# Weight sums by DMA issued in a pinned order, with 2048 bytes of scratch for dynamic DMAs

## The chip, the core and the metric

The kernel runs on one core of a Trainium2 chip, in one launch. TensorE (PE) multiplies, VectorE (DVE) and ScalarE (ACT) work elementwise, GpSimd (POOL) does small things and issues some DMAs, SyncE (SP) issues the others; all transfers of the core run on the same 16 DMA engines. The metric is the device time of one execution in microseconds, as the median of several runs. Times below that look like clock readings ("at 242.62") are microseconds from the start of the profiled span.

## What is computed

Two layers of a decoder trunk on 512 tokens of width 1024. Each layer is a feed-forward block, a mixer (attention and retention) and a second feed-forward block, each followed by a layer norm. All arithmetic is float32. The change is in the feed-forward block, which runs four times:

```python
def swiglu_ffn(x, w_gu, w_down):
    a, u = jnp.split(x @ w_gu, 2, axis=-1)
    return (jax.nn.silu(a) * u) @ w_down
...
for l in range(DEPTH):
    x = layer_norm(DEEPNORM_ALPHA * x + 0.5 * swiglu_ffn(x, ffn1_w_gu[l], ffn1_w_down[l]),
                   ln1_g[l], ln1_b[l])
    x = layer_norm(DEEPNORM_ALPHA * x + hybrid_mixer(...), ln2_g[l], ln2_b[l])
    x = layer_norm(DEEPNORM_ALPHA * x + 0.5 * swiglu_ffn(x, ffn2_w_gu[l], ffn2_w_down[l]),
                   ln3_g[l], ln3_b[l])
```

The hidden width (`D_FF`) is 2816, so `w_down` is 2816 x 1024.

## The kernel before

**Precision.** Every operand is split in a rounded high part and a rest: ACT casts the high part (L159, tiles `uh` for weights, `hh` for activations), DVE subtracts it from the source (L160, `ul` and `hl`). A product is then three matmuls on PE (L168 to L170: high by high, high by low, low by high). ACT and DVE each take their instructions in the order in which they stand in the program.

**Weights.** They come by DMA from SP into two buffers `raw`, are split into one of six pairs of buffers (`uh`, `ul`), and are used once. The class `Weights` holds a list of items, one for each pair, and runs up to six items ahead of the matmuls. Which instruction stands where on an engine is then settled by a scheduler when the program is built, except for those that are pinned by `keep_in_program_order`.

**The down projection.** A part of `x @ w_down` is done by a scheme with seven instead of eight block products (Strassen's). It is made of seven steps, each with two halves, one for each of two groups of rows, g = 0 and 1; a half is 12 matmuls. Some steps use a sum of blocks of `w_down` instead of a block. These sums are made by the DMA engines: the two buffers `R[0]` and `R[1]` (one for each group, which reuse the two `S` buffers of the stage ahead) have two halves x = 0 and 1 of 512 KB. SP loads a block into each (L356), and POOL then issues DMAs that add another block onto what is there (`add`, L349, `accum_op=ALU.add`). For each group there are three additions onto half 0, one after the other, and one onto half 1:

- half 0: first sum (used by step 3), second sum (step 4), third sum (step 7). Each addition after the first has to wait until the split of the sum before it (`cut`, ACT L159 `uh<-R`, then DVE L160 `ul<-R`) has read the buffer.
- half 1: its one sum is used by step 6.

So there are eight additions in a feed-forward block, 32 in all, and eight splits of `R`. The texts below number them as they stand on POOL: before the change, additions 1 to 8 are g0 first, g0 half 1, g1 first, g1 half 1, g0 second, g1 second, g0 third, g1 third. Splits 1 to 8 are, on ACT and DVE: first sums of g0 and g1, second sums, halves 1, third sums. The left operand of step 3 is made by `fifth` (L640 to L649), once for each group: DVE subtracts (L645), ACT casts (`hh<-s`), DVE subtracts the rest (`hl<-s`). On ACT the cast for group 1 stands behind split 4.

**POOL** does nothing else around this place. Its other work is a power for each layer norm (L458) and things of the mixer. A DMA that POOL issues is described by POOL in memory set aside for it, `dynamic_dma_scratch_size` bytes in each partition (L1113). The small statistics of norms, attention and retention lie in the pool `small` (L105), with four buffers for each name.

Of the kernel before, what the change touches and what calls it, by code (L numbers as in the profile page):

```python
# [10 lines left out]
ALU = mybir.AluOpType  # L11
# [28 lines left out]
class Weights:  # L40


    def __init__(self, T, items):
        self.T, self.items = T, items
        self.emitted = self.taken = self.out = 0
        self.ready = []
        self.raws = {}
        self.last = {raw: i for i, (raw, _, _, _) in enumerate(items)}
# [44 lines left out]
class Trunk:  # L93
    def __init__(self, tc, ctx):
        self.tc, self.nc = tc, tc.nc
        self.n = 0
        self.now = 0
        self.pin = True
        self.tasks = []
        self.later = []  # L100
        nc = self.nc
        self.base = ctx.enter_context(tc.tile_pool(name="base", bufs=1))
        self.rawp = ctx.enter_context(tc.tile_pool(name="rawp", bufs=2))
        self.unit = ctx.enter_context(tc.tile_pool(name="unit", bufs=UBUFS))
        self.small = ctx.enter_context(tc.tile_pool(name="small", bufs=4))  # L105
        self.psum = ctx.enter_context(tc.tile_pool(name="psum", bufs=8, space=PSUM))
        self.ident = self.base.tile([P, P], F32, name="ident")
        make_identity(nc, self.ident)
        self.mhalf = self.base.tile([P, 8], F32, name="mhalf")
        nc.vector.memset(self.mhalf, -0.5)  # L110
        self.xh = self.base.tile([P, KC, SEQ], F32R, name="xh")
        self.xl = self.base.tile([P, KC, SEQ], F32R, name="xl")
        self.Y = self.base.tile([P, NT, D], F32, name="Y")
# [226 lines left out]
    def down_items(self, w, key, R, row):  # L340

        def block(i, j, g):
            r0 = i * 512 + g * 256
            return w[r0 : r0 + 256, j * 512 : (j + 1) * 512].rearrange("(k p) c -> p k c", p=P)

        def add(g, x, i, j):
            self.nc.gpsimd.dma_start(R[g][:, x], block(i, j, g), accum_op=ALU.add)  # L349

        def begin(go):
            def f(v, hi, lo):
                for g in range(2):
                    R[g] = self.spool.tile([P, 2, 2, 512], F32, tag="S", name=self.nm("R"), bufs=2)
                    for x in range(2):
                        self.nc.sync.dma_start(R[g][:, x], block(0, x, g))  # L356
                    add(g, 0, 0, 1)
                return go(v, hi, lo)
            return f

        def cut(g, x, *after):
            def go(v, hi, lo):
                hv, lv = (t.rearrange("p (k c) -> p k c", k=2) for t in (hi, lo))
                self.split(hv, lv, R[g][:, x])
                for a in after:
                    add(g, *a)
                return hv, lv
            return (None, None, None, go)

        p1, p2, p3 = (self.wide_item(w, j * 512, i, (key, "b", i, j)) for i, j in ((0, 0), (1, 0), (1, 1)))  # L370
        p1[0] = p1[0][:3] + (begin(p1[0][3]),)
        return (p1 + p2 + [cut(g, 0, (0, 1, 1), (1, 1, 1)) for g in range(2)]
                + [cut(g, 0, (0, 1, 0)) for g in range(2)] + p3 + [cut(g, 1) for g in range(2)]
                + [row] + [cut(g, 0) for g in range(2)])

# [751 lines left out]
```

## Time and profile before

| | |
|---|---|
| time, median of 3 runs | 1902.52 us (1901.39 to 1902.53) |
| the profiled execution, its own time | 1903.95 us |
| its span in the trace | 1902.2 us |
| mean granted TensorE clock | 0.981 |
| busy: PE, DVE, ACT, POOL | 96%, 71%, 46%, 7% |
| additions by DMA (L349) in a row, each feed-forward block | 8, the first at 226.1, 806.3, 1169.3 and 1747.7 |

The span runs from the first to the last instruction in the trace; the execution's own time is 1.75 us longer. PE is busy nearly all the time, so that what matters is the few places where it waits, and the clock that it is granted there. A row of the timeline gives the start, the duration, the engine, the line, the operation, output and input, how many instructions are merged, and in brackets how long the engine had been idle and what ended that. A row of the chain of work that ended last gives a start, a duration and what was done; "issue" is time in which the engine waited for nothing that the profile shows. A row of the waits gives the microseconds in total, the number of times and the longest.

### The profile page before, as it was taken

The numbers are of one execution on the slowest core, as the hardware profiler recorded it, in microseconds if no ns is written. First come the engines' busy times: TensorE is split into PE (matmuls) and PEld (weight loads), VectorE is DVE, ScalarE is ACT, GpSimd is POOL, SyncE is SP. The second block draws the span as 40 slices with busy tenths as digits, with TensorE's granted clock in tenths as the row PEclk, the third lists the DMA queues.
The fourth block names the chain that finished last, engine by engine and source line by source line (L and its number), as shares of the span: only waits on it lengthen the run. The fifth ranks groups of instructions, "written<-read, shape, count | busy, mean of one in ns | idle before, by whom it ended". The sixth has DMA issues, their size and how long they took to land.

```text
span 1902.2 us, 29290 instructions
## 1 busy us (share of the span) xinstructions
PE 1823.9 (96%) x12074; PEld 1657.7 (87%) x12074; DVE 1341.5 (71%) x1942; ACT 879.6 (46%) x1439; POOL 124.3 (7%) x104
## 2 busy tenths in 40 slices
PE   9999969999999999969999999699999999999698
PEld 9999958897789999958899999588877899999586
DVE  7788756655758788756688887646567687887655
ACT  4455534168623455534235554432785234555330
POOL 0000010110110000010000000101111100000101
PEclk9999989999999999989999999899999999999899
DMA  5242564232222223365322236541232122425631
GB/s 177 89 134 90 160 130 168 74 95 79 55 89 81 97 89 126 120 148 173 99 66 91 90 105 190 127 155 62 78 90 89 45 89 91 132 89 166 140 116 45
DMA packets 151989, 205.87 MB, mean 108 GB/s; under 512 B 4656, under 2 KB 116016, under 8 KB 151856
## 3 DMA queue, kind: packets, MB, share of 16 engines
q1 hardware_dynamic: 143152, 187.23, 30.4%
q0 software_dynamic: 8704, 16.78, 5.5%
q8 instruction: 94, 1.54, 0.3%
q14 instruction: 39, 0.32, 0.1%
HBM read 201.89 MB, written 2.10 MB: 107 GB/s over the span
## 4 chain that ended last, share of the span: by engine, by line
PE 77%; issue 10%; DVE 5%; DMA 3%; ACT 2%; POOL 2%; SPq 0%; POOLq 0%; DVEq 0%; ACTq 0%
PE ps L170 25%; PE ps L169 25%; PE ps L168 25%; DMA R<-in_ffn_w_down_dram 1%; ACT sw L896 1%; POOL sw L898 1%; DMA raw<-in_ffn_w_gu_dram 1%; POOL R L349 1%; PE ps L426 1%; DVE Y L462 1%; DVE st L452 1%; DVE ul L160 1%; ACT uh L159 1%; DVE Y L459 1%; DVE Y L450 0%
## 5 line engine op out<-in xcount | busy, mean ns | idle before, releaser
L168 PE MATMUL ps<-xh,uh 128*128 128x256 f32 (+1 forms) x1616 | 482.7, 299 | 0.7 <-ACT uh L159 0.7
L169 PE MATMUL ps<-xl,uh 128*128 128x256 f32 (+1 forms) x1616 | 480.0, 297 | 0.6 <-DVE xl L160 0.6
L170 PE MATMUL ps<-xh,ul 128*128 128x256 f32 (+1 forms) x1616 | 479.7, 297 | 0.4 <-DVE ul L160 0.4
L159 ACT CAST uh<-raw 128x1024 fp32r<-128x1024 f32 (+1 forms) x325 | 291.1, 912 | 229.7 <-PE ps L169 149.3
L160 DVE TENSOR_TENSOR ul<-raw,uh 128x1024 fp32r<-128x1024 f32 (+1 forms) x325 | 336.7, 1049 | 83.5 <-ACT uh L159 83.0
L170 PE MATMUL ps<-Th,ul 128*128 128x256 f32 x1152 | 326.0, 283 | 0.0
L168 PE MATMUL ps<-Th,uh 128*128 128x256 f32 x1152 | 326.0, 283 | 0.0
L169 PE MATMUL ps<-Tl,uh 128*128 128x256 f32 x1152 | 326.0, 283 | 0.0
L168 PEld LDWEIGHTS ps<-xh,uh 128*128 128x128 f32 x1616 | 309.3, 191 | 11.1 <-issue 1.6
L170 PEld LDWEIGHTS ps<-xh,ul 128*128 128x128 f32 x1616 | 309.1, 191 | 9.2 <-DVE ul L160 0.8
L169 PEld LDWEIGHTS ps<-xl,uh 128*128 128x128 f32 x1616 | 309.3, 191 | 8.7 <-DVE xl L160 1.2
L168 PE MATMUL ps<-uh,hh 128*128 128x512 f32 x640 | 254.5, 398 | 56.4 <-ACT hh L159 56.4
L170 PE MATMUL ps<-uh,hl 128*128 128x512 f32 x640 | 254.1, 397 | 5.5 <-DVE hl L160 5.5
L169 PE MATMUL ps<-ul,hh 128*128 128x512 f32 x640 | 253.1, 395 | 0.0
L160 DVE TENSOR_TENSOR ul<-S,uh 128x1024 fp32r<-128x1024 f32 x144 | 175.8, 1221 | 72.8 <-ACT uh L159 72.4
L159 ACT CAST uh<-S 128x1024 fp32r<-128x1024 f32 x144 | 151.0, 1048 | 160.5 <-PE ps L169 159.2
L168 PEld LDWEIGHTS ps<-Th,uh 128*128 128x128 f32 x1152 | 221.2, 192 | 0.0
L169 PEld LDWEIGHTS ps<-Tl,uh 128*128 128x128 f32 x1152 | 221.2, 192 | 0.0
L170 PEld LDWEIGHTS ps<-Th,ul 128*128 128x128 f32 x1152 | 221.2, 192 | 0.0
L168 PEld LDWEIGHTS ps<-uh,hh 128*128 128x128 f32 x640 | 122.9, 192 | 83.3 <-ACT hh L159 58.1
L170 PEld LDWEIGHTS ps<-uh,hl 128*128 128x128 f32 x640 | 122.4, 191 | 35.4 <-DVE hl L160 10.1
L169 PEld LDWEIGHTS ps<-ul,hh 128*128 128x128 f32 x640 | 122.7, 192 | 25.6
(141 smaller groups left out, 2248.5 us busy)
## 6 DMA issues: line engine op xcount, KB each, us to landing
raw<-in_ffn_w_gu_dram SPq DMA_DIRECT2D x86, 1024.0 KB, 5.5
raw<-in_ffn_w_down_dram SPq DMA_DIRECT2D x40, 1024.0 KB, 5.1
raw<-in_w_in_dram SPq DMA_DIRECT2D x18, 1024.0 KB, 5.4
R<-in_ffn_w_down_dram POOLq DMA_DIRECT2D x32, 512.0 KB, 6.0
R<-in_ffn_w_down_dram SPq DMA_DIRECT2D x16, 512.0 KB, 5.9
raw<-in_w_in_dram SPq DMA_DIRECT2D x8, 512.0 KB, 5.1
raw<-in_w_out_dram SPq DMA_DIRECT2D x8, 512.0 KB, 6.1
raw<-in_w_out_dram SPq DMA_DIRECT2D x4, 1024.0 KB, 5.0
```

The lines of the kernel that those rows point to most:

```text
L159: a = self.nc.scalar.copy(hi, src)
L160: b = self.nc.vector.tensor_sub(lo, src, hi.bitcast(F32))
L168: mm(out, ah, bh, start=start, stop=False, **kw)
L169: mm(out, ah, bl, start=False, stop=False, **kw)
L170: mm(out, al, bh, start=False, stop=stop, **kw)
L349: self.nc.gpsimd.dma_start(R[g][:, x], block(i, j, g), accum_op=ALU.add)
L426: nc.tensor.transpose(b[:, c * P : (c + 1) * P], src[:, c * P : (c + 1) * P], self.ident)
L452: nc.vector.bn_stats(out=st[:, h, :], in_=y[:, hs])
L459: nc.vector.scalar_tensor_tensor(out=y, in0=y, scalar=mv[:, 0:1], in1=g, op0=ALU.subtract, op1=ALU.mult)
L462: nc.vector.scalar_tensor_tensor(out=y[:, hs], in0=y[:, hs], scalar=rs, in1=b[:, hs], op0=ALU.mult, op1=ALU.add)
L896: nc.scalar.copy(sw[q * 32 : q * 32 + 32, :n], src[o * 32 : o * 32 + 32, :n])
L898: nc.gpsimd.tensor_mul(sw[:, :n], sw[:, :n], S)
```

## The change

- Each addition is pinned behind what stands before it on POOL's queue (`keep_in_program_order`).
- The additions onto half 1 are written with the first ones, ahead of all splits, and no longer behind split 1 and split 2.
- The scratch for dynamic DMAs grows from 1024 to 2048 bytes in each partition, and the pool `small` has three buffers for each name, no longer four.

```diff
-        self.small = ctx.enter_context(tc.tile_pool(name="small", bufs=4))
+        self.small = ctx.enter_context(tc.tile_pool(name="small", bufs=3))
...
         def add(g, x, i, j):
-            self.nc.gpsimd.dma_start(R[g][:, x], block(i, j, g), accum_op=ALU.add)
+            self.tc.keep_in_program_order(self.nc.gpsimd.dma_start(R[g][:, x], block(i, j, g), accum_op=ALU.add))
...
                     add(g, 0, 0, 1)
+                for g in range(2):
+                    add(g, 1, 1, 1)
                 return go(v, hi, lo)
...
-        return (p1 + p2 + [cut(g, 0, (0, 1, 1), (1, 1, 1)) for g in range(2)]
+        return (p1 + p2 + [cut(g, 0, (0, 1, 1)) for g in range(2)]
                 + [cut(g, 0, (0, 1, 0)) for g in range(2)] + p3 + [cut(g, 1) for g in range(2)]
...
-    nc = _bacc.Bacc("TRN2", target_bir_lowering=False, num_devices=1, dynamic_dma_scratch_size=1024)
+    nc = _bacc.Bacc("TRN2", target_bir_lowering=False, num_devices=1, dynamic_dma_scratch_size=2048)
```

On POOL, in the first feed-forward block, these rows stood before the change (`R_2638` is the buffer of group 0, `R_2642` that of group 1; a row with x2 is two additions in a row, onto half 0 and onto half 1):

```order
L349 DMA R_2638<-in_ffn_w_down_dram 128x2x512 x2
L349 DMA R_2642<-in_ffn_w_down_dram 128x2x512 x2
L349 DMA R_2638<-in_ffn_w_down_dram 128x2x512
L349 DMA R_2642<-in_ffn_w_down_dram 128x2x512
L349 DMA R_2638<-in_ffn_w_down_dram 128x2x512
L349 DMA R_2642<-in_ffn_w_down_dram 128x2x512
L458 TENSOR_TENSOR rs_3494<-ve_3492,mhalf 128x1
```

The scheduler had thus already put the additions onto half 1 ahead of the second sums. With the change the same place on POOL reads:

```order
L349 DMA R_2638<-in_ffn_w_down_dram 128x2x512
L349 DMA R_2642<-in_ffn_w_down_dram 128x2x512
L349 DMA R_2638<-in_ffn_w_down_dram 128x2x512
L349 DMA R_2642<-in_ffn_w_down_dram 128x2x512
L349 DMA R_2638<-in_ffn_w_down_dram 128x2x512
L349 DMA R_2642<-in_ffn_w_down_dram 128x2x512
L349 DMA R_2638<-in_ffn_w_down_dram 128x2x512
L349 DMA R_2642<-in_ffn_w_down_dram 128x2x512
L460 TENSOR_TENSOR rs_3494<-ve_3492,mhalf 128x1
```

One pair has changed places: the first sum of group 1 is now the second addition, and half 1 of group 0 the third. The additions 4 to 8 stand where they stood. The other three blocks read in the same way.

On ACT, at the splits of `R` in the first block, these rows stood before (`uh<-R` are splits 1 to 4, `hh<-s_328` the casts of `fifth`):

```order
L159 CAST uh_2770<-R_2638 128x1024
L159 CAST hh_2792<-hT_145 128x512
L159 CAST hh_2796<-hT_145 128x512
L159 CAST hh_2818<-s_328_2791 128x512
L159 CAST uh_2812<-R_2642 128x1024
L159 CAST uh_2837<-R_2638 128x1024
L159 CAST uh_2842<-R_2642 128x1024
L159 CAST hh_2849<-s_328_2791 128x512
L159 CAST uh_2868<-raw_2679 128x1024
```

And with the change:

```order
L159 CAST uh_2772<-R_2638 128x1024
L159 CAST hh_2793<-hT_145 128x512
L159 CAST hh_2797<-hT_145 128x512
L159 CAST hh_2818<-s_328_2792 128x512
L159 CAST uh_2813<-R_2642 128x1024
L159 CAST uh_2837<-R_2638 128x1024
L159 CAST uh_2842<-R_2642 128x1024
L159 CAST hh_2849<-s_328_2792 128x512
L159 CAST uh_2868<-raw_2681 128x1024
```

Nothing has moved here but numbers in names, nor has anything on DVE, PE or SP in the whole program: POOL's pair is the only difference in order.

## The prediction

> **What bounds the kernel now.** PE is busy 96% of the span, so I began with what PE waits for. The view of waits, for PE, is headed by these rows:
>
> ```profile
> PE ps L168 <- ACT hh L159: 56.4, 4, 14.3
> PE ps L170 <- DVE hl L160: 5.5, 8, 1.3
> ```
>
> Four waits of about 14.1 us, one in each feed-forward block, are nearly all that PE waits. Next I read the chain of work that ended last, at the first of them (start, duration, what):
>
> ```profile
> 240.79 1.22 DVE ul L160
> 242.01 0.61 DVE hl L160
> 242.62 1.21 POOL R L349
> 243.83 5.13 issue
> 248.98 1.23 POOL R L349
> 250.21 4.99 issue
> 255.22 1.21 POOL R L349
> 256.43 5.05 issue
> 261.50 5.95 DMA R<-in_ffn_w_down_dram
> 267.53 1.05 ACT uh L159
> 268.60 1.23 DVE ul L160
> ...
> 270.43 0.61 DVE hl L160
> 271.09 0.79 PE ps L170
> ```
>
> The chain is four additions by DMA in single file (additions 3, 4, 5 and 6), then split 4, then PE. Why PE waits for an `hh` cast is seen on ACT (its timeline):
>
> ```profile
> 248.74 1.05 ACT L159 CAST uh<-R 128x1024 fp32r<-128x1024 f32 x1 [6.59 <-DMA R<-in_ffn_w_down_dram]
> ...
> 268.48 0.61 ACT L159 CAST hh<-s 128x512 fp32r<-128x512 f32 x1
> ```
>
> The cast of group 1 for step 3 stands behind splits 3 and 4 and cannot start until addition 6 has landed, though step 3 itself needs only first sums. So the time at which addition 6 lands sets the end of the wait.
>
> What holds the additions apart? Two pairs of starts on POOL's timeline, in the first and in the second block, and how long the earlier of each pair took from issue to landing (the DMA view of windows 232:233 and 813:814):
>
> ```profile
> 226.13 1.35 POOL L349 DMA_DIRECT2D R<-in_ffn_w_down_dram  x1 [224.82 <-DVE Q L530]
> 232.47 1.23 POOL L349 DMA_DIRECT2D R<-in_ffn_w_down_dram  x1 [4.99 <-issue]
> ...
> 813.64 1.23 POOL L349 DMA_DIRECT2D R<-in_ffn_w_down_dram  x1 [6.14 <-DMA R<-in_ffn_w_down_dram]
> 821.84 1.21 POOL L349 DMA_DIRECT2D R<-in_ffn_w_down_dram  x1 [6.98 <-issue]
> ```
>
> ```profile
> R<-in_ffn_w_down_dram POOLq DMA_DIRECT2D x1, 512.0 KB, 9.9
> ```
>
> ```profile
> R<-in_ffn_w_down_dram POOLq DMA_DIRECT2D x1, 512.0 KB, 7.9
> ```
>
> 232.47 + 9.9 = 242.4, and addition 3 starts at 242.62; 813.64 + 7.9 = 821.5, and the next starts at 821.84. Each addition starts 0.2 to 0.3 us after the one before it has landed, whether that took 6 or 10 us, and also where its own data had long been there (addition 4 needs only a plain load). I read this as room for one addition in the scratch: the next can be described only when the last is done.
>
> **The change part by part.** The scratch doubles. If one addition fits in 1024 bytes and two don't, at least two fit in 2048, and additions overlap. The trace of before has no two in flight, so the new pitch is bounded. The queues' totals:
>
> ```profile
> q1 hardware_dynamic: 143152, 187.23, 30.4%
> q0 software_dynamic: 8704, 16.78, 5.5%
> ```
>
> 32 additions took 5.5% of 16 engines over 1902.2 us, 3.3 us each; the other loads 30.4% of the span for 187 MB, 3.1 us for each MB. These are the pitches if the engines are what limits. The 3.3 us hold the slow start of a lone transfer, which in a queue lies beside its predecessor's tail; I take 2.9.
>
> The order changes too: group 1's first sum goes from third to second. It needs SP's plain load of that half (SP's timeline, and the DMA view of window 227.4:227.8):
>
> ```profile
> 227.52 0.91 SPq L356 DMA_DIRECT2D R<-in_ffn_w_down_dram  x2
> ```
>
> ```profile
> R<-in_ffn_w_down_dram SPq DMA_DIRECT2D x1, 512.0 KB, 6.0
> ```
>
> That lands at 233.5, so the new addition 2 starts near 233.8, against 232.47 for today's. Today's took 9.9 us beside a raw load and landed at 242.4; I take 242.6 for the new one, 6 us ahead of where group 1's first sum now lands (242.62 + about 6.0 = 248.6). Split 2 then runs near 242.7, not at 248.74. Additions 3 and 4 (half 1) have their data and are issued at once or as room comes free; addition 5 needs split 1, whose DVE part ends at 242.0 (first row of the chain) and doesn't move; addition 6 needs split 2, about 1.05 + 1.23 us behind 242.7, so 245.0. From then on the engines decide. They have, after 242.6, the rest of SP's next raw load, and additions 3, 4, 5 and 6:
>
> ```profile
> 239.15 0.37 SPq L265 DMA_DIRECT2D raw<-in_ffn_w_down_dram  x1
> ```
>
> I give the rest of this 1 MB 2.3 of its 3.1 us. Addition 6 lands at 242.6 + 2.3 + 4 x 2.9 = 256.5, against 267.5 now: **11.0 us earlier**. Bounds: with 3.3 and 3.1 in full, 258.9, so 8.6 us earlier; from below, so early that PE never waits.
>
> From landing to PE everything stays: 267.5 to 271.1 is 3.6 us (ACT, DVE, DVE), so PE resumes at 260.1. Is it there by then? PE's wait of 14.3 us ended as ACT's cast did, at 269.1, so it began at 254.8, and PE had lost 1.3 us just before, in one of the waits of the second row of the view of waits, for split 2's late data, which falls away. So PE arrives at 253.5 and still waits until 256.5 + 1.7 = 258.2: 4.7 us, where it was 14.3. The saving is 11.0 us in a block. The four waits are alike (56.4 / 4 = 14.1), so **44 us** for four.
>
> Then the clock. The windows of PE's idle time and the 10 us behind it, first and second block (the number behind POOL's count is the granted clock):
>
> ```profile
> 254.90:269.10 14.20, 0.00 (x0) 0.00 (x0) 3.52 (x5) 2.62 (x4) 3.65 (x3) 0.66 0.48 74
> 269.10:279.10 10.00, 9.23 (x26) 6.88 (x27) 9.96 (x13) 5.62 (x8) 1.22 (x1) 0.63 0.67 123
> 833.90:848.00 14.10, 0.00 (x0) 0.00 (x0) 3.51 (x5) 2.60 (x4) 3.62 (x3) 0.59 0.49 74
> 848.00:858.00 10.00, 9.22 (x30) 7.04 (x31) 10.00 (x13) 6.61 (x9) 1.21 (x1) 0.73 0.66 146
> ```
>
> A mean of 0.66 over 14.2 us, of 1.0 and 0.5, says that the clock fell 4.5 us after PE stopped, and 0.59 that it fell after 2.5 us. Behind the wait 0.63 and 0.73 are 7.4 and 5.4 us at half speed, of which about 1.3 are PE's short second wait: 3 and 2 us lost, 2.5 in a block, 10 in all. With 4.7 us of idle time left the clock sits at the edge of falling; I count half of it gone, **5 us**. [...]
>
> DVE is busy 9.96 of the 10 us behind the wait. Its work there is a backlog that the late sums made, and it will now be spread over the time when DVE is idle (3.52 us busy of 14.2); what would be late next is DVE's `hl` for the steps behind, at up to 1.3 us a time (the second row of waits). I take nothing for it and keep 4 x 1.3 = 5 us for the range.
>
> The pins cost no instruction. Three buffers in `small` could make a norm wait for the third one before it; the nearest row is DVE's wait for POOL's power in a norm:
>
> ```profile
> DVE Y L462 <- POOL rs L458: 3.6, 8, 0.5
> ```
>
> Half a microsecond at the longest, and a norm's statistics are done with before the next two are; nothing. The additions onto half 1 and SP's loads have slack: split 5 stands on ACT behind split 4, so a half-1 sum ready anywhere before 256 is early.
>
> The sum against the profiled execution's own time, 1903.95 us (its span of 1902.2 and 1.75 around it): 1903.95 - 44 - 5 = 1855. The median of the runs is 1.4 us lower, so I say **1854 us**.
>
> **The rivals.**
>
> *No wait is left* (0.10). If additions pass each other faster than 2.2 us apart, addition 6 lands by 252 and PE never stops: 56.4 + 5.5 of waits and 10 of clock go, 1902.5 - 72 = 1831. For it: a lone addition's 5.9 us are mostly latency if the rate of plain loads is the measure. Against it: 3.3 us of engine time each.
>
> *Engines at full price, and the clock falls each time* (0.18). Pitch 3.3 us, 8.6 us saved in a block, none of the clock: 1902.5 - 34 = 1868; with 5 us of DVE's lateness, 1873.
>
> *The scratch is not what serialises* (0.08). If POOL waits for its last addition for another reason, additions stay 6.2 us apart, and the swap alone brings addition 6 no earlier, since it is sixth in both orders: 1902.5. For it: nothing in the trace names the scratch; the gap is only "issue". Against it: the gap follows the landing in all cases. [...]
>
> *Single file, and later* (0.05), the slower side. In single file, the new addition 2 waits on POOL for SP's load of group 1, at the head of the queue, while addition 3, whose data is there, stands behind it: 233.8 against 232.47, 1.3 us that every later addition inherits, addition 6 with them. 4 x 1.3 = 5.3 us: 1908. It decides only if no two additions overlap, as with two in flight the 11 us outweigh it.
>
> **How the numbers follow.** The forecast (a wait of some 5 us is left, clock in between) has 0.59, and 1854. The range has to hold it and the two cases at its sides: from 1832 to 1874, which leaves out the two cases without overlap (0.13) and a little at the ends. A measurement of this kernel can tell about 0.2% (3.8 us) from no change. Faster by more than that are the first three cases, 0.87; within it the scratch rival, 0.08; slower the last, 0.05.
>
> **What would show it.** Right: POOL's starts of additions 2 to 4 come 1.2 to 6 us apart and ahead of the landing of the one before; split 2 on ACT near 242.7; addition 6 lands near 256.5; PE's four waits for `hh` are 3 to 6 us; the clock's low time shrinks. Wrong: starts still 0.3 us behind the last landing (scratch), or landings more than 3.3 us apart with two in flight (pitch), or new waits of PE on `hl` behind step 3 (DVE).

## The result, and the profile after

| | before | after |
|---|---|---|
| time, median of 4 runs each | 1901.95 us (1899.06 to 1902.53) | 1839.62 us (1839.41 to 1840.85) |
| ratio to before, 95% interval | | 0.9677 (0.966 to 0.9693) |
| span of the profiled execution | 1902.2 us | 1837.8 us |
| mean granted TensorE clock | 0.981 | 0.991 |

The kernel is 62 us faster; 1854 was predicted, 48 us faster than 1902.5. The time lies inside the range and beside the forecast by 14 us. One of the runs of the kernel before that stand beside the experiments below fell into a slower state (2541.25 us at a granted clock of 0.653) and is left out of the comparisons. Three views say where the 62 us came from. First PE's waits, after (total, times, longest):

```profile
PE ps L168 <- ACT hh L159: 16.0, 4, 4.3
PE ps L170 <- DVE hl L160: 4.8, 4, 1.6
```

The four waits for the cast are still there, but last 4.0 us each (14.1 before). The two rows together fell from 61.9 to 20.8 us: 41.1 us. POOL's timeline after, at the additions of the second block, shows why (a row with x3 is three additions in a row):

```profile
791.46 3.69 POOL L349 DMA_DIRECT2D R<-in_ffn_w_down_dram  x3 [7.40 <-DMA R<-in_ffn_w_down_dram]
798.13 1.20 POOL L349 DMA_DIRECT2D R<-in_ffn_w_down_dram  x1 [2.98 <-DVE ul L160]
802.40 1.19 POOL L349 DMA_DIRECT2D R<-in_ffn_w_down_dram  x1 [3.07 <-DVE hl L160]
```

Additions 2, 3 and 4 are issued within 3.7 us without a gap; before, each began 0.2 to 0.3 us behind the landing of the last. Most of the waits is thus accounted for, but 41 is not 62. PE's windows from 100 to 200 us, inside the first block's gate and up products, long before any addition, before and after (busy time and number of matmuls):

```profile
100.00:200.00 100.00, 100.00 (x836) 100.00 (x835) 83.96 (x125) 52.71 (x80) 0.00 (x0) 1.00 0.32 103
```

```profile
100.00:200.00 100.00, 100.00 (x862) 100.00 (x861) 86.91 (x130) 54.45 (x82) 0.00 (x0) 1.00 0.34 107
```

PE is never idle here, and its clock is 1.00 in both. Yet after the change it does 862 matmuls instead of 836: one every 116.0 ns, not every 119.6. The groups of PE's instructions with different shapes kept apart tell which kind it is, before and then after (total in us, mean of one in ns):

```profile
L168 PE MATMUL ps<-xh,uh 128*128 128x256 f32 x1408 | 399.4, 284 | 0.7 <-ACT uh L159 0.7
...
L168 PE MATMUL ps<-Th,uh 128*128 128x256 f32 x1152 | 326.0, 283 | 0.0
```

```profile
L168 PE MATMUL ps<-xh,uh 128*128 128x256 f32 x1408 | 398.6, 283 | 0.2 <-ACT uh L159 0.2
...
L168 PE MATMUL ps<-Th,uh 128*128 128x256 f32 x1152 | 319.1, 277 | 0.0
```

Products with `Th` and `Tl` (sums of blocks of x, in the seven-product scheme) became 6 ns shorter each; the same product with `xh` hardly changed (284 and 283 ns). PE's order and the code of these matmuls are the same in both kernels. What the change does move is where tiles lie: three buffers in `small` in place of four, and 1024 more bytes of scratch, shift everything behind them in a partition. By the allocation, `Th` starts 111,872 bytes behind the weight buffer `uh` before, a multiple of 128, and 111,552 after, 64 off a multiple of 128. `xh` lies 65,536 bytes ahead of `uh` in both.

So there are two theories of the 62 us. **Mine, as predicted:** all of it comes from the additions, whose share was then mis-sized. **The rival:** some 42 us come from the scratch, and some 20 from where the tiles lie, which `small` moves.

### The profile page after: what moved, and what is told of

Read it like the earlier page. It is cut to its first block, busy times and chain, and to the rows that moved or that the text cites. A ratio compares the mean times of both kernels' runs of the same rounds, so it can differ in the third digit from the quotient of the medians.

```text
span 1837.8 us, 29295 instructions
## 1 busy us (share of the span) xinstructions
PE 1801.7 (98%) x12074; PEld 1634.5 (89%) x12074; DVE 1341.4 (73%) x1942; ACT 880.5 (48%) x1439; POOL 123.8 (7%) x104
## 4 chain that ended last, share of the span: by engine, by line
PE 81%; DVE 5%; issue 5%; ACT 4%; DMA 3%; POOL 1%; SPq 0%; POOLq 0%; DVEq 0%; ACTq 0%
PE ps L170 26%; PE ps L168 26%; PE ps L169 26%; DMA R<-in_ffn_w_down_dram 2%; ACT sw L898 1%; PE ps L428 1%; DVE ul L160 1%; DMA raw<-in_ffn_w_gu_dram 1%; ACT uh L159 1%; ACT b L940 1%; ACT b L934 1%; DVE Y L464 1%; POOL sw L900 1%; DVE st L454 1%; DVE Y L461 0%
## 5 line engine op out<-in xcount | busy, mean ns | idle before, releaser
L168 PE MATMUL ps<-Th,uh 128*128 128x256 f32 x1152 | 319.1, 277 | 0.0
L169 PE MATMUL ps<-Tl,uh 128*128 128x256 f32 x1152 | 318.7, 277 | 0.0
L170 PE MATMUL ps<-Th,ul 128*128 128x256 f32 x1152 | 318.3, 276 | 0.0
L160 DVE TENSOR_TENSOR ul<-S,uh 128x1024 fp32r<-128x1024 f32 x144 | 175.9, 1222 | 62.3 <-ACT uh L159 61.7
L168 PEld LDWEIGHTS ps<-Th,uh 128*128 128x128 f32 x1152 | 216.7, 188 | 0.0
L169 PEld LDWEIGHTS ps<-Tl,uh 128*128 128x128 f32 x1152 | 216.7, 188 | 0.0
L170 PEld LDWEIGHTS ps<-Th,ul 128*128 128x128 f32 x1152 | 216.3, 188 | 0.0
```

What stands on the lines that cost most here:

```text
L160: b = self.nc.vector.tensor_sub(lo, src, hi.bitcast(F32))
L168: mm(out, ah, bh, start=start, stop=False, **kw)
L169: mm(out, ah, bl, start=False, stop=False, **kw)
L170: mm(out, al, bh, start=False, stop=stop, **kw)
```

## The experiments

**Each part by itself.** `e1` is the kernel before with three buffers in `small` and nothing else:

```diff
-        self.small = ctx.enter_context(tc.tile_pool(name="small", bufs=4))
+        self.small = ctx.enter_context(tc.tile_pool(name="small", bufs=3))
```

> The kernel before, with three buffers in the pool of small tiles and nothing else: scratch 1024, additions in the old order, so that only the feed-forward tiles behind that pool lie 320 bytes lower (in the change they lie 704 higher, again 320 less than the weight tiles). Theory 'two gains' (the scratch shortens PE's four waits, and the place of the tiles speeds up the gate-up matmuls): 1881 to 1886 us, the Th matmuls start 113 to 114 ns apart and not 120, PE's four waits stay at 14.1 us. Rival 'one gain' (the matmuls are faster because of the scratch or of the shorter waits): 1900 to 1904 us, 120 ns.

`e2` is the changed kernel with four buffers in `small`, and scratch of 1920 bytes so that it fits; the distances between tiles are then those of before:

```diff
-        self.small = ctx.enter_context(tc.tile_pool(name="small", bufs=3))
+        self.small = ctx.enter_context(tc.tile_pool(name="small", bufs=4))
...
-    nc = _bacc.Bacc("TRN2", target_bir_lowering=False, num_devices=1, dynamic_dma_scratch_size=2048)
+    nc = _bacc.Bacc("TRN2", target_bir_lowering=False, num_devices=1, dynamic_dma_scratch_size=1920)
```

> The changed kernel with four buffers of small tiles and 1920 bytes of scratch: pins and order as changed, all tiles 896 bytes higher than before, so that tiles and weights lie to each other as before. Theory 'two gains': 1855 to 1860 us (about 45 us less than before), Th matmuls 120 ns apart, additions overlap as in the changed kernel and PE's waits are 4 us. Rival 'one gain': 1838 to 1842 us, 113 ns.

`e3` is the kernel before with both numbers of the change, but neither pins nor new order:

```diff
-        self.small = ctx.enter_context(tc.tile_pool(name="small", bufs=4))
+        self.small = ctx.enter_context(tc.tile_pool(name="small", bufs=3))
...
-    nc = _bacc.Bacc("TRN2", target_bir_lowering=False, num_devices=1, dynamic_dma_scratch_size=1024)
+    nc = _bacc.Bacc("TRN2", target_bir_lowering=False, num_devices=1, dynamic_dma_scratch_size=2048)
```

`e4` is the reverse, the changed kernel with both numbers of before:

```diff
-        self.small = ctx.enter_context(tc.tile_pool(name="small", bufs=3))
+        self.small = ctx.enter_context(tc.tile_pool(name="small", bufs=4))
...
-    nc = _bacc.Bacc("TRN2", target_bir_lowering=False, num_devices=1, dynamic_dma_scratch_size=2048)
+    nc = _bacc.Bacc("TRN2", target_bir_lowering=False, num_devices=1, dynamic_dma_scratch_size=1024)
```

> The kernel before with 2048 bytes of scratch and three buffers of small tiles, additions in the old order and not pinned (first sum of group 1 third). Theory 'the scratch is what serialised them': additions overlap, the first sum of group 1 lands one pitch (3 to 4 us) later than in the changed kernel, the sixth addition at about the same time or up to 3 us later; 1840 to 1852 us. Rival 'the order is what helps': additions in single file still, PE's waits 14 us, 1881 to 1886 us from the place of the tiles alone.

> The kernel before with the pins and the new order alone: scratch 1024, four buffers of small tiles. Theory 'the scratch is what serialised them': single file, each start 0.3 us behind the last landing, the sixth addition lands 0 to 1.5 us later than before; 1901 to 1908 us. Rival 'the order is what helps': PE's waits shrink by several us, below 1885 us.

The four ran beside the kernel before at 1900.29 us, the median of twelve runs:

| | time, us | ratio, 95% interval | PE's wait for `hh`, 4 times |
|---|---|---|---|
| e1, `small` alone | 1881.98 | 0.9906 (0.9891 to 0.9921) | 54.7 |
| e2, all but `small` | 1858.23 | 0.9777 (0.9761 to 0.9794) | 15.0 |
| e3, scratch and `small` | 1836.87 | 0.9668 (0.9653 to 0.9682) | 14.0 |
| e4, order and pins alone | 1899.90 | 1.0 (0.999 to 1.0009) | 59.4 |

The first row of PE's waits of `e1`, and one group of its matmuls:

```profile
PE ps L168 <- ACT hh L159: 54.7, 4, 13.9
```

```profile
L168 PE MATMUL ps<-Th,uh 128*128 128x256 f32 x1152 | 319.1, 277 | 0.0
```

The same two rows of `e2`:

```profile
PE ps L168 <- ACT hh L159: 15.0, 4, 5.3
```

```profile
L168 PE MATMUL ps<-Th,uh 128*128 128x256 f32 x1152 | 326.2, 283 | 0.0
```

`e1` has the short matmuls and the long waits, `e2` the short waits and the long matmuls. `e1` saves 18.3 us and `e2` 42.1, together 60.4 of the 62.3 between the medians. `e3` has both gains without the new order and the pins (it even came 3 us below the range expected of it), and `e4` has order and pins and gains nothing. The rival theory stands: the scratch is worth some 42 us, the place of tiles some 18, the order nothing that these runs can tell.

**How many additions does the scratch hold?** In `e4`, with 1024 bytes, POOL's timeline and the DMA view at 242.0 to 242.2 show single file:

```profile
242.06 1.21 POOL L349 DMA_DIRECT2D R<-in_ffn_w_down_dram  x1 [6.68 <-issue]
248.25 1.23 POOL L349 DMA_DIRECT2D R<-in_ffn_w_down_dram  x1 [4.98 <-issue]
```

```profile
R<-in_ffn_w_down_dram POOLq DMA_DIRECT2D x1, 512.0 KB, 5.9
```

242.06 + 5.9 = 247.96, and the next starts 0.3 us later. With 2048 bytes there are three at a time: in the rows of after above, additions 2 to 4 are in flight together, addition 5 begins behind the landing of the first of them, and addition 6 begins at 802.40. The DMA view of after at 791.4 to 793 gives the three a median of 9.9 us, which is that of addition 3 (issued about 792.2):

```profile
R<-in_ffn_w_down_dram POOLq DMA_DIRECT2D x3, 512.0 KB, 9.9
```

792.2 + 9.9 = 802.1, 0.3 us ahead of 802.40. `e10` is `e5`, told of further down, with 1536 bytes:

```diff
-    nc = _bacc.Bacc("TRN2", target_bir_lowering=False, num_devices=1, dynamic_dma_scratch_size=2048)
+    nc = _bacc.Bacc("TRN2", target_bir_lowering=False, num_devices=1, dynamic_dma_scratch_size=1536)
```

> As e5, but with 1536 bytes of scratch in place of 2048; no distance between operands changes. Theory A (an addition takes between a third of 2048 and half of 1536 bytes): two in flight, the third starts about 0.3 us behind the landing of the first of them; the second sums, which stand behind the two first sums, are hardly later, 1812 to 1822 us. Theory B (an addition takes more than half of 1536): single file again, starts 0.2 to 0.3 us behind the last landing, g1 second lands some 4 us later, and waits of 2 to 5 us a block come back, 1824 to 1842 us.

Its POOL timeline in the second block, and the DMA view at 792.0 to 792.2:

```profile
792.08 1.20 POOL L349 DMA_DIRECT2D R<-in_ffn_w_down_dram  x1 [5.64 <-DVE ul L160]
795.02 1.21 POOL L349 DMA_DIRECT2D R<-in_ffn_w_down_dram  x1 [1.74 <-DVE ul L160]
799.09 1.20 POOL L349 DMA_DIRECT2D R<-in_ffn_w_down_dram  x1 [2.85 <-issue]
```

```profile
R<-in_ffn_w_down_dram POOLq DMA_DIRECT2D x1, 512.0 KB, 6.7
```

Two are in flight, and the third starts 0.3 us behind the landing of the first (792.08 + 6.7 = 798.8). `e2` has 1920 bytes, and its POOL timeline shows three issued in a row there too, of which the first took 7.9 us to land (the DMA view at 233.6 to 233.7):

```profile
233.65 3.70 POOL L349 DMA_DIRECT2D R<-in_ffn_w_down_dram  x3 [6.34 <-DVE Q L547]
```

One in 1024, two in 1536 and three in 1920 bytes: by these counts an addition takes more than 512 and at most 640 bytes (an estimate from them). What of an addition lies there, no run shows.

**What is left of the waits.** In POOL's order after the change, additions 5 and 6 (the second sums, on which splits 3 and 4 wait) stand behind two additions onto half 1 that nobody needs yet, and these share the DMA engines with them: the DMA view of after at 227 to 241.2 has 60.6% of the 16 engines' time on additions, and gives the five issued there a median of 10.0 us to landing, where a lone one of before took 5.9 (the DMA view of before at 248 to 249.5). `e5` takes the changed kernel and writes these two behind the second sums, pinned (first sums, second sums, halves 1, third sums):

```diff
-                for g in range(2):
-                    add(g, 1, 1, 1)
                 return go(v, hi, lo)
...
                 for a in after:
-                    add(g, *a)
+                    add(*a)
...
-        return (p1 + p2 + [cut(g, 0, (0, 1, 1)) for g in range(2)]
-                + [cut(g, 0, (0, 1, 0)) for g in range(2)] + p3 + [cut(g, 1) for g in range(2)]
+        return (p1 + p2 + [cut(0, 0, (0, 0, 1, 1)), cut(1, 0, (1, 0, 1, 1), (0, 1, 1, 1), (1, 1, 1, 1))]
+                + [cut(g, 0, (g, 0, 1, 0)) for g in range(2)] + p3 + [cut(g, 1) for g in range(2)]
```

> The changed kernel with the additions pinned in another order: first sums, second sums, halves 1, third sums. Theory A (the PE waits that are left, about 4.0 and 1.1 us in a block, come from the two additions onto half 1 that run ahead of the second sums and share the engines with them): addition g1 second lands before about 246 in the first block (249.44 in the changed kernel), PE's wait for the hh cast shrinks from 4 to 0 to 1.5 us a block, the clock stays at full speed there, and the time is 1808 to 1822 us. Theory B (the second sums are bound by their own chain: first sum, split, addition, and by the raw loads of SP beside them, so that the place of halves 1 does not matter): waits of 3.5 to 4.3 us stay, 1836 to 1843 us. Theory C (halves 1 now come too late for split 5): waits of the same size at step 6, over 1836 us.

1813.68 us (1811.82 to 1814.12), ratio 0.9545 (0.9532 to 0.9558): 26 us below the changed kernel. ACT's timeline of the changed kernel at splits 3 and 4 and the cast of step 3:

```profile
247.00 1.05 ACT L159 CAST uh<-R 128x1024 fp32r<-128x1024 f32 x1 [9.24 <-DMA R<-in_ffn_w_down_dram]
249.51 1.05 ACT L159 CAST uh<-R 128x1024 fp32r<-128x1024 f32 x1 [1.47 <-DMA R<-in_ffn_w_down_dram]
250.53 0.62 ACT L159 CAST hh<-s 128x512 fp32r<-128x512 f32 x1
```

The same of `e5`:

```profile
242.05 1.05 ACT L159 CAST uh<-R 128x1024 fp32r<-128x1024 f32 x1 [4.96 <-DMA R<-in_ffn_w_down_dram]
244.76 1.05 ACT L159 CAST uh<-R 128x1024 fp32r<-128x1024 f32 x1 [1.66 <-DMA R<-in_ffn_w_down_dram]
245.72 0.62 ACT L159 CAST hh<-s 128x512 fp32r<-128x512 f32 x1
```

The cast comes 4.8 us sooner, ahead of PE, which reaches step 3 near 247.4 in both. The first row of PE's waits of `e5` is now the short one for DVE:

```profile
PE ps L170 <- DVE hl L160: 4.8, 4, 1.6
```

About 16 us of waits went; the other 10 are for the most part the clock. The windows of PE's first wait and the 10 us behind it, after (first and second block, with the granted clock behind POOL's count):

```profile
247.44:251.20 3.76, 0.00 (x0) 0.00 (x0) 3.12 (x5) 2.29 (x4) 1.20 (x1) 0.81 0.29 52
251.20:261.20 10.00, 8.92 (x29) 6.74 (x30) 10.00 (x13) 6.39 (x8) 1.22 (x1) 0.73 0.97 209
809.02:812.97 3.95, 0.00 (x1) 0.00 (x1) 3.13 (x5) 2.46 (x4) 1.20 (x1) 1.00 0.27 49
812.97:822.97 10.00, 8.93 (x27) 6.67 (x28) 9.96 (x13) 5.74 (x8) 1.21 (x1) 0.66 0.97 209
```

And of `e5`, first block:

```profile
247.43:248.56 1.13, 0.00 (x1) 0.00 (x1) 1.13 (x3) 1.13 (x2) 0.84 (x1) 1.00 1.08 194
248.56:258.56 10.00, 10.00 (x44) 8.21 (x45) 10.00 (x13) 5.54 (x9) 0.38 (x1) 1.00 0.96 229
```

After a stop of 3.8 to 4.0 us PE runs at half clock (granted 0.50 from 251.2 to 255.0 in after, as from 260.0 to 275.0 before) for 5.4 to 6.8 of the next 10 us, of which about 1.1 are its second wait: some 2.5 us lost in a block, nearly as much as before the change. After 1.13 us it runs on at full clock. Where the limit lies can't be said: in `e8`, told of further down, PE stopped for 1.55 us in the second and in the third block, and in the 10 us behind, the clock held in the one and fell in the other:

```profile
791.28:792.83 1.55, 0.00 (x0) 0.00 (x0) 1.55 (x4) 1.55 (x3) 0.85 (x1) 1.00 1.12 201
792.83:802.83 10.00, 10.00 (x44) 8.22 (x45) 10.00 (x13) 5.41 (x9) 0.37 (x1) 1.00 0.88 216
1128.84:1130.39 1.55, 0.00 (x1) 0.00 (x0) 1.55 (x4) 1.55 (x3) 0.84 (x1) 1.00 1.08 198
1130.39:1140.39 10.00, 10.00 (x37) 8.06 (x38) 10.00 (x13) 5.47 (x9) 0.38 (x1) 0.83 0.91 223
```

`e10` is `e5` with less scratch, at 1814.12 us (0.9552, 0.9535 to 0.9569): with the additions in this order, two in flight do as well as three.

**The place of the tiles.** Two kernels put 64 unused bytes into the changed kernel. `e6` has them between `xh`, `xl`, `Y` and the weights, so that `uh` moves away from `xh` and takes `Th` along; in `e7` the same line stands ahead of `ident`, the first of all tiles, so that everything moves together.

```diff
         self.Y = self.base.tile([P, NT, D], F32, name="Y")
+        self.pad = self.base.tile([P, 16], F32, name="pad")
```

> The changed kernel with 64 unused bytes between the tiles xh, xl, Y and the weight tiles uh, ul, so that uh, ul and Th, Tl lie 64 bytes higher and xh, xl stay. Theory A (a 128x256 matmul starts 120 ns behind the last when its two operands lie a multiple of 128 bytes apart, and 113 ns when they lie 64 off): matmuls with Th stay at 113 (still 64 off uh) and those with xh go from 120 to 113 (now 64 off uh); 1818 to 1829 us. Theory B (what counts is the address of the moving operand alone, 32 above a multiple of 128 slow, 96 above fast): Th goes back to 120 and xh stays at 120; 1855 to 1862 us. Theory C (neither): no change, 1836 to 1843 us.

> The changed kernel with 64 unused bytes ahead of all tiles, so that everything lies 64 bytes higher and no distance between operands changes. Theory A (distance between the two operands counts): matmul starts stay 113 ns apart with Th and 120 with xh; 1836 to 1843 us. Theory B (address of the moving operand counts, modulo 128): Th goes to 120, xh to 113; between 1838 and 1848 us as the two nearly balance, but the steps of the two kinds swap.

`e6` took 1819.63 us (0.9577, 0.9564 to 0.959), `e7` 1839.00 us (0.968, 0.9666 to 0.9693). The two groups of matmuls in `e6` (all lines of this kernel stand one lower):

```profile
L169 PE MATMUL ps<-xh,uh 128*128 128x256 f32 x1408 | 391.0, 278 | 0.3 <-ACT uh L160 0.3
...
L169 PE MATMUL ps<-Th,uh 128*128 128x256 f32 x1152 | 318.0, 276 | 0.0
```

And in `e7`:

```profile
L169 PE MATMUL ps<-xh,uh 128*128 128x256 f32 x1408 | 398.7, 283 | 0.1
...
L169 PE MATMUL ps<-Th,uh 128*128 128x256 f32 x1152 | 319.1, 277 | 0.0
```

In `e7` the addresses of `xh` and `Th` modulo 128 have changed places (by the allocation 32 and 96 after, 96 and 32 in `e7`), no distance has changed, and neither have the two groups; in `e6` `xh` stands where it did, only `uh` has moved, and the products with `xh` became shorter. In these two runs it is thus the distance between the two operands that counts, not the address of the moving one. Is any distance but a multiple of 128 as good? `e9` has 32 unused bytes in place of 64 (`[P, 8]`):

> As e6, but with 32 unused bytes in place of 64, so that xh lies 32 off uh (modulo 128) and Th stays 64 off. Theory A (only a multiple of 128 is slow): matmuls with xh start 113 ns apart, 1818 to 1826 us. Theory B (the operands must be a full 64 off): xh stays at 120, 1836 to 1843 us. Th stays at 113 by both.

1842.62 us (0.9703, 0.9686 to 0.9721), with this group:

```profile
L169 PE MATMUL ps<-xh,uh 128*128 128x256 f32 x1408 | 396.7, 282 | 0.4 <-ACT uh L160 0.4
```

Both theories fell in part: `xh` gained 1 ns where 64 off gained it 5, and `Th`, still 64 off, rose from 277 to 278 ns; PE does 860 matmuls between 100 and 200 us, 862 after. So 64 off is the good one of the three distances tried. The two slow distances, 65,536 and 111,872, are multiples of 256 as well, so whether a distance of 128 more would be slow isn't shown. Whether `Th` lost its 1 ns to its new address or to the products with `xh` that run between, wasn't tried; the rule behind it stays open.

**Both together.** `e8` has the order of `e5` and the 64 bytes of `e6`; `e11` the same with 1536 bytes of scratch.

> The changed kernel with the second sums ahead of halves 1 (as in e5) and 64 unused bytes between xh, xl, Y and the weight tiles (as in e6). Theory A (the two are separate costs): their gains over the changed kernel add up, 1839.6 - 26 - 20 = 1794 us, 1789 to 1800; no wait of PE for the hh cast, and steps of 113 ns both with Th and with xh. Theory B (faster matmuls bring PE to step 3 sooner, so that additions that just came in time are late again): waits of 0.5 to 2 us a block come back, 1797 to 1806 us.

> As e8, but with 1536 bytes of scratch, so that two additions are in flight and not three. The five times of e8 lay 14 us apart (1792.56 to 1806.64) at granted clocks of 0.995 to 0.999. Theory A (the spread comes from three additions in flight beside other loads, which is settled anew in each execution): times within 4 us, 1791 to 1797. Theory B (the spread belongs to the matmuls in their new places, or to loads that PE now overtakes, and not to the scratch): again more than 8 us between the lowest and the highest, 1792 to 1808. With 512 bytes less, everything lies 512 bytes lower and no distance between operands changes.

`e8` took 1799.55 us (1792.56 to 1806.64), ratio 0.9481 (0.9453 to 0.9508); `e11` 1794.62 us (1793.61 to 1802.22), ratio 0.9451 (0.9434 to 0.9468). Both beat every other kernel here. The lowest times are what the gains give when added up (1794), but the times scatter by 9 to 14 us. They do so also with two additions in flight, though there four of the five lie within 3.4 us; three in flight are thus not needed for a late time. The profiled execution of `e11` was its slowest, that of `e8` its fastest. PE's window of the first block's products in `e8`:

```profile
60.00:220.00 160.00, 160.00 (x1414) 160.00 (x1414) 137.99 (x203) 89.12 (x135) 1.35 (x1) 1.00 0.36 116
```

The windows of the first and the second block's in `e11`:

```profile
60.00:220.00 160.00, 160.00 (x1361) 160.00 (x1360) 135.72 (x201) 85.98 (x130) 0.00 (x0) 1.00 0.33 109
620.00:780.00 160.00, 160.00 (x1414) 160.00 (x1413) 136.79 (x202) 89.36 (x136) 2.47 (x2) 1.00 0.38 121
```

1414 matmuls in 160 us are 113.2 ns each, 1361 are 117.6. In this execution these products ran at the slower pace in the first block and not in the second, on the same addresses; 53 matmuls of 113 ns are 6 us of the 9.6 between the spans of the two executions (1800.4 and 1790.8). What decides the pace of a block was not found. `e11` also has a wait for the `hh` cast again, in its second block alone, and the clock fell behind it (the first row of the two windows is the wait, the second the 10 us behind it):

```profile
PE ps L169 <- ACT hh L160: 2.3, 1, 2.3
```

```profile
798.11:800.38 2.27, 0.00 (x2) 0.00 (x1) 2.27 (x5) 1.67 (x3) 1.19 (x1) 1.00 0.96 144
800.38:810.38 10.00, 8.83 (x26) 6.59 (x27) 9.96 (x13) 5.66 (x8) 2.42 (x2) 0.66 1.04 188
```

The wait of theory B of `e8` has thus come back in one block of this execution, be it that PE was there sooner or that an addition took longer; in `e8`'s trace it is 0.3 us. What the slower executions that were not profiled had of each is not known.

## Why the prediction was right in direction and short in size

- **What bounds the kernel** held: four waits of PE for the `hh` cast, set by the landing of addition 6 (`e2`: 56.4 us of them became 15.0).
- **The scratch serialises the additions** held (`e4`: single file, with order and pins changed; `e3`: short waits, with the scratch and `small` alone). "At least two fit" was three.
- **The time of addition 6.** The changed kernel can't be laid beside the forecast of 256.5, since PE reaches the place some 7 us sooner (247.4, not 254.9). `e2`, which has the matmuls of before, can: addition 2 began at 233.65 (233.8 forecast), addition 6 landed at 254.4, 246.07 and 8.3 us to landing (256.5), and PE stood from 253.00 to 256.17 (253.5 to 258.2). Addition 5, issued at 242.13, took 9.8 us and landed at 251.9 (the DMA view at 242.1 to 242.3), so the last two landed 2.5 us apart: the pitch of 2.9 us was a little dear.
- **The clock term, 5 us,** was wrong, and is about 0. In the prediction's own rows PE is busy 9.23 and 9.22 of the 10 us behind the wait, so its second wait there is 0.8 us, not the 1.3 that was taken off, and the loss before was 3.3 and 2.3 us in the two blocks. It stayed about as large. The granted clock over the 3.17 us of the first wait of `e2` and the 10 us behind it:

```profile
253.00:256.17 3.17, 0.00 (x2) 0.00 (x1) 3.13 (x5) 1.69 (x4) 1.20 (x1) 1.00 0.18 32
256.17:266.17 10.00, 8.70 (x26) 6.46 (x27) 9.96 (x13) 5.60 (x8) 1.22 (x1) 0.66 0.97 210
```

  At 0.66 that is 6.8 us at half speed, less 1.3 of waits, and so 2.8 us lost; behind the second wait of `e2`, of 5.27 us, the 10 us were granted 0.60. What went is the low time in which PE stood. The clock fell even behind this short wait of 3.17 us, so half a term for half the idle time had no basis.
- **DVE's backlog** was put at nothing, with 5 us kept for it in the range. PE's second wait grew from 0.8 us in the first block to 1.2 as the mean of four (4.8 in `e2`), some 2 us in all.
- **The swap of additions** has no price of its own in the sum, and is worth nothing (`e4`: 0.999 to 1.0009). The pins: nothing. The slower rival ("single file, and later", 1908) would have needed additions that don't overlap; where they don't, in `e4`, new addition 2 began 1.7 us later than before, but took 7.6 us and not 9.9, so that it landed at 241.8 (242.4 before), and nothing was lost that the runs can tell.
- **"Three buffers in `small` ... nothing"** is the step that failed. I asked only whether a norm would wait for a buffer; the norms' wait for POOL is 3.6 us in all, as before. The buffers' bytes, though, decide where each later tile lies, and that was worth 18.3 us by itself (`e1`), with an interval of 15 to 21.

So 44 + 5 for the additions measured 42.1 (`e2`), all of it waits (61.9 to 19.8 us in the first two rows), and 0 for the tiles measured 18.3. The first miss hid some of the second: the sum came out 14 us short, in a part of the program that I had not looked at, since no instruction of it changes. That the time still lay inside the range was luck as far as the tiles go, since the range was made for the additions.

## What to carry to other kernels

A change in the size of a pool moves the tiles behind it (here by 320 bytes, `e1`); before a gain is put down to the part that one meant to change, compare a stretch that it can't have touched (here PE's count of matmuls between 100 and 200 us), and try the moved tiles by themselves. Where DMAs with an addition follow each other at their landing plus a constant (0.2 to 0.3 us before), the size of the scratch is the first thing to try (1024 to 2048 bytes took 45 us off between `e1` and `e3`), and then what stands in the queue ahead of the transfer that is waited for. A short stop of PE that costs it the clock can be worth more than its length: here 16 us less of waits brought 26 (`e5`).

## What the runs showed of the hardware that was not expected

- Matmuls of 128x256 in this kernel follow each other at 113 or at 120 ns (113.2 in the first block of `e8`, 119.6 before, at 100 to 200 us), by the distance of their two operands in a partition (64 off a multiple of 128 bytes, or 0 off); 32 off gave a mean of 282 ns for one matmul (`e9`), between 278 (`e6`) and 283 (after). The longer matmuls (128x512) of `xh` did not gain by 64 off (401 ns after, 404 in `e6`).
- Where all operands lie 64 off, these matmuls of one block ran at 117.6 ns and those of another at 113.2, in the same execution of `e11` (1361 and 1414 in 160 us).
- One addition of 512 KB by DMA was in flight with 1024 bytes of scratch in each partition (`e4`), two with 1536 (`e10`), three with 1920 (`e2`) and with 2048 (after, issued within 3.7 us); by that one takes between 513 and 640 bytes (an estimate from these counts).
- The clock fell behind a stop of 3.2 us that one of 1.3 us followed (`e2`), and not behind one of 1.1 us alone (`e5`); behind one of 1.55 us it fell in one block of `e8` and not in another.
